# Hybrid decoder layer on one core: three more seven-product pairs in the down projection, part of their block sums made earlier and kept in DRAM, and another order at the end

## The chip, the cores and the metric

One core of one Trainium2 chip. The metric is the device time of one launch in microseconds (us), the median of 3 runs. Engines are called PE (matrix multiply; PEld is its weight load), DVE (vector), ACT (scalar), POOL and SP (the engine whose queue issues nearly all transfers).

## The reference

One decoder layer on x of 256 x 2048 float32, with 16 heads of 128 columns in two groups:

```python
h    = rmsnorm(x, pre_mix_gain)
proj = h @ w_in                                  # 2048 x 6144: q, k, v of 16 heads
o    = concat(stick_breaking(8 heads), dilated(8 heads))   # each head rms-normed
x    = x + rmsnorm(o @ w_out, post_mix_gain)
h    = rmsnorm(x, pre_ffn_gain)
u    = h @ w_up                                  # 2048 x 11008
u    = sum(up[:, j:j + S] * conv_w[j] for j in range(3)) + conv_b     # causal, depthwise
gate, val = split(u)
x    = x + rmsnorm((gelu(gate) * val) @ w_down, post_ffn_gain)        # w_down: 5504 x 2048
```

All is float32, so each matrix is split into a high part (a rounded copy) and a low part (what the rounding left), and a product is three matmuls: high by high, low by high, high by low.

## The kernel before, in words

The weights come as a list of chunks of two tiles of 128x1024 (512 KB each), through five `raw` buffers that SP fills in the list's order. `high` (L88) makes the high part of a tile on ACT, `low` (L93) the low part on DVE by subtracting; there are four buffers for each of the two parts. The chunks are worked in stages: for each of four head groups four value chunks and eight query/key chunks (with the attention of the heads between them), then the output projection, a transition (residual, norm, transposes), 86 chunks of up (43 blocks of 128 columns, gate and value, with convolution and GeLU in `convolved`, L448), and down.

Down (`class Down`, L483) contracts over 43 blocks of 128 rows of w_down, once for each half `cp` of the 2048 output columns. A single block with its 1024 columns is one tile and four products (`ONE`): 12 matmuls of 128x512. Two neighbouring blocks can be a **pair**: a 2x2 block product in the manner of Strassen and Winograd, with seven products for eight (`PAIR`): 21 matmuls for 24. For that it needs sums of y's blocks (made in `convolved` during up) and of the weight's blocks. Of the weight's four 128x512 blocks, tile `ra` holds b12 and b21, tile `rb` the other two, side by side. The sums are T13 = b12 + rb (128x1024, L542) and T24 (two sums of 128x512, L543 and L544, from T13, rb and b21). A pair is then four *units*, each to be split by ACT and DVE and multiplied by PE: T13, T24 and Rb (128x1024, two products each) and Ra (128x512, one product).

`_down_plan` (L40) sets the order. With `NPAIR = 10` there are 10 pairs and 23 singles: in the first half 2 singles, then the pairs with 17 singles spread behind them, then 4 singles; in the second half no single ahead, 19 spread, and the last 4 (`HELD`) are prepared and multiplied at the very end, bank by bank. `run` (L585) prepares (`prepare`, L529: load, sums, high, low) three units ahead of the one that it multiplies. `combine` and `close` add up the seven PSUM banks into `fg`.

The end of `run` takes the last four singles bank by bank. A finished bank is added to `fg` on DVE (`close`, L581), its squares are summed on ACT (`squares`, L397), and it is multiplied by the gain ("take", L583, on POOL or DVE). When the row mean is there (`mean`, L407 to L410; `newton`, L416 and L418), `put` (L616) scales, adds the residual x1b and stores a piece of the output. Rows 0 to 127 are ready first (`put(0, ...)`), rows 128 to 255 (`put(1, ...)`) last.

Each engine executes its own list of instructions in order; a scheduler sets that order from the program and its buffers, except where `pin` keeps the program's order. In the transition `update` (L707) adds the residual in pieces of 128x512, and PE transposes them (L715).

The functions that the change touches:

## Time and profile before

| | |
|---|---|
| runs | 1132.15, 1132.9, 1133.07 us: median 1132.9 |
| the profiled execution | 1131.0 us, of it 1129.2 us from the first to the last instruction |
| busy | PE 1111.9, DVE 856.5, ACT 645.6, POOL 6.3 us |
| clock that PE was granted | 0.996 of full speed over the span |
| transfers | 216.86 MB, 192 GB/s over the span |

The span is from the first to the last instruction of the profiled execution; its own time lies 1.8 us above that, and it was 1.9 us below the median of the runs. Engines run side by side, so busy times don't add up; what an engine's idle time costs depends on whether PE waits for it. The stages stand in the span so: head groups and output projection to about 400 us, the transition to about 410, up to about 893, down from 893 on, and from 1118.7 the end without PE.

### The profile page before, as it was taken

The page shows a single profiled execution, that of the slowest core. Times are in us where ns is not written, and L with a number is a line of the kernel's source. Part 1 is how long each engine was busy: PE and PEld are TensorE (multiplying, and loading weights), DVE is VectorE, ACT ScalarE, POOL GpSimd, SP SyncE. Part 2 cuts the span into 40 slices and gives each one's busy share as a digit, 9 for nine tenths or more (in the row PEclk, how much of TensorE's full clock was granted, in tenths as well). Part 3 has the DMA queues.
Part 4 walks back from the last instruction along what each step waited for, and adds up shares of the span by engine and source line. Part 5 has one row for each costly group of instructions (what it writes and reads, how often), then busy time and mean ns, then how long its engine had stood idle before and what let it go on. Part 6 is the DMA issues. An engine that isn't in the chain of part 4 may idle for free.

```text
span 1129.2 us, 16027 instructions
## 1 busy us (share of the span) xinstructions
PE 1111.9 (98%) x5873; PEld 946.5 (84%) x5873; DVE 856.5 (76%) x1336; ACT 645.6 (57%) x1037; POOL 6.3 (1%) x12
## 2 busy tenths in 40 slices
PE   8999999999999999999999999999999999999996
PEld 6888888888888888888888888888888878887885
DVE  6665565765755488788888887888888898898986
ACT  7555564655654386555555555555555555564563
POOL 0000000000000000000000000000000000000001
PEclk9999999999999999999999999999999999999999
DMA  9764545555555556555555555555555455566555
GB/s 362 250 211 160 186 150 167 169 161 179 165 168 188 185 190 206 187 190 187 188 185 192 184 193 186 189 183 189 186 188 187 153 208 202 204 204 219 208 189 186
DMA packets 59551, 216.86 MB, mean 192 GB/s; under 512 B 6737, under 2 KB 7121, under 8 KB 58705
## 3 DMA queue, kind: packets, MB, share of 16 engines
q1 hardware_dynamic: 59184, 215.77, 57.4%
q8 instruction: 46, 0.75, 0.3%
q14 instruction: 33, 0.26, 0.1%
q10 hardware_dynamic: 288, 0.07, 0.0%
HBM read 211.63 MB, written 4.19 MB: 191 GB/s over the span
## 4 chain that ended last, share of the span: by engine, by line
PE 94%; DVE 3%; ACT 1%; DMA 1%; issue 1%; DVEq 0%; ACTq 0%
PE mmu L101 28%; PE mmu L104 14%; PE mmqk L101 10%; PE p L563 6%; PE p L561 5%; PE p L562 5%; PE mmqk L104 5%; PE mmo L138 3%; PE mmo L134 3%; PE mmo L135 3%; PE mmv L134 3%; PE mmv L135 2%; PE mmv L138 2%; DMA raw<-in_w_v 1%; DVE wl L93 1%
## 5 line engine op out<-in xcount | busy, mean ns | idle before, releaser
L93 DVE TENSOR_TENSOR wl<-raw,wh 128x1024 fp32r<-128x1024 f32 (+1 forms) x387 | 457.8, 1192 | 203.0 <-ACT wh L88 199.8
L88 ACT CAST wh<-raw 128x1024 fp32r<-128x1024 f32 (+1 forms) x387 | 394.2, 1026 | 343.4 <-PE mmu L101 194.5
L101 PE MATMUL mmu<-hT,wh 128*128 128x512 f32 x1344 | 340.5, 395 | 0.2 <-ACT wh L88 0.2
L101 PEld LDWEIGHTS mmu<-hT,wh 128*128 128x128 f32 x1344 | 240.8, 188 | 45.0 <-ACT wh L88 0.4
L104 PEld LDWEIGHTS mmu<-hT,wl 128*128 128x128 f32 x1344 | 184.1, 188 | 15.3
L104 PE MATMUL mmu<-hT,wl 128*128 128x256 f32 x1344 | 187.4, 281 | 0.0
L101 PE MATMUL mmqk<-hT,wh 128*128 128x512 f32 x512 | 132.9, 400 | 0.0
L101 PEld LDWEIGHTS mmqk<-hT,wh 128*128 128x128 f32 x512 | 92.0, 188 | 17.1
L88 ACT CAST wh<-room 128x1024 fp32r<-128x1024 f32 x40 | 42.0, 1050 | 70.3 <-DVE room L542 41.0
L104 PEld LDWEIGHTS mmqk<-hT,wl 128*128 128x128 f32 x512 | 70.0, 188 | 5.8
L563 PE MATMUL p<-wl,yt 128*128 128x512 f32 (+1 forms) x188 | 72.8, 388 | 0.0
L562 PE MATMUL p<-wh,yt 128*128 128x512 f32 (+1 forms) x188 | 72.6, 386 | 0.0
L561 PE MATMUL p<-wh,yt 128*128 128x512 f32 (+1 forms) x188 | 72.6, 386 | 0.0
L104 PE MATMUL mmqk<-hT,wl 128*128 128x256 f32 x512 | 71.2, 281 | 0.0
L563 PE MATMUL p<-wl,yp 128*128 128x512 f32 x140 | 54.8, 395 | 1.0 <-DVE wl L93 1.0
L561 PE MATMUL p<-wh,yp 128*128 128x512 f32 x140 | 55.0, 393 | 0.4 <-ACT wh L88 0.3
L562 PE MATMUL p<-wh,yp 128*128 128x512 f32 x140 | 54.8, 391 | 0.0
L134 PE MATMUL mmv<-wh,hT 128*128 128x512 f32 x128 | 51.7, 406 | 1.5 <-ACT hT L215 1.0
L455 ACT ACTIVATE cv<-u,par 128x256 f32<-128x256 f32 x86 | 51.4, 599 | 2.1 <-DVE u L453 2.1
L93 DVE TENSOR_TENSOR wl<-room,wh 128x1024 fp32r<-128x1024 f32 x40 | 48.8, 1221 | 4.4 <-ACT wh L88 3.6
L135 PE MATMUL mmv<-wh,hT 128*128 128x512 f32 x128 | 50.7, 396 | 0.3 <-DVE hT L236 0.3
L134 PE MATMUL mmo<-wh,mix 128*128 128x512 f32 x128 | 50.6, 396 | 0.0
(173 smaller groups left out, 1223.1 us busy)
## 6 DMA issues: line engine op xcount, KB each, us to landing
raw<-in_w_up SPq DMA_DIRECT2D x172, 512.0 KB, 4.4
raw<-in_w_dn SPq DMA_DIRECT2D x86, 512.0 KB, 4.3
raw<-in_w_qk SPq DMA_DIRECT2D x64, 512.0 KB, 4.1
raw<-in_w_o SPq DMA_DIRECT2D x32, 512.0 KB, 3.6
raw<-in_w_v SPq DMA_DIRECT2D x31, 512.0 KB, 3.7
x<-in_x SPq DMA_DIRECT2D x2, 1024.0 KB, 9.4
x_kept<-x SPq DMA_DIRECT2D x2, 1024.0 KB, 4.4
x1b<-x_kept SPq DMA_DIRECT2D x4, 512.0 KB, 5.3
```

The costliest lines, as they stand in the source:

```text
L88: pin(A.copy(wh, raw))
L93: pin(V.tensor_tensor(wl, raw, wh.bitcast(F32), op=ALU.subtract))
L101: T.matmul(ps, wh[:, j * P:(j + 1) * P], h[:, k, :, :], start=(k == 0), stop=False, skip_group_check=True)
L104: T.matmul(ps[:, 0, :], wl[:, j * P:(j + 1) * P], h[:, k, 0, :], start=False, stop=(k == KT - 1), skip_group_check=True)
L134: T.matmul(ps[t], hi[:, k, tc_], ws, start=(first and i == 0 and j == 0), stop=False)
L135: T.matmul(ps[t], lo[:, k, tc_], ws, start=False, stop=False)
L138: T.matmul(ps[t], hi[:, k, tc_], wl[:, j * 512:(j + 1) * 512], start=False, stop=(last and i == len(parts) - 1 and j == n - 1))
L455: A.activation(cv, u, AF.Identity, scale=cw(2), bias=par[:, P_CB + f:P_CB + f + 1])
L561: T.matmul(ps, yh, wh[:, cs], start=key not in self.begun, stop=False)
L562: T.matmul(ps, yl, wh[:, cs], start=False, stop=False)
L563: T.matmul(ps, yh, wl[:, cs], start=False, stop=self.left[key] == 0)
```

## The change

It has five parts.

1. `NPAIR` is 13, with 17 singles. In the first half 11 singles are spread over 13 pairs (none behind the first and the seventh), in the second half 13 over 13.
2. `presum` is called in each query/key chunk, 26 times. It loads b12 (256 KB) and the pair's other two blocks (512 KB) of w_down, adds them on DVE (128x1024, L535), and stores the result, T13, in DRAM (512 KB, `t13_kept`), one chunk after the sum. Down then loads three tiles for each pair, T13, rb and b21, where it loaded two, and makes only T24's sums (L563, L564), after T13's split.
3. In `convolved` the sums of y's blocks lie in seven rows in another order, so that one cast and one subtraction of 128x896 take the place of two each.
4. `u` and `cv` have single buffers in up, and small tiles move between pools.
5. The end: the takes of the first two banks are made on DVE, those of the last but one and of half of the last on POOL; the residual of rows 0 to 127, columns 1024 to 2047, is copied to PSUM by ACT (`x1p`) and read there; the pieces of `put` for row block 0 are 1024, 256, 256, 512; the order is pinned. In the transition the first update of the second row block is made in two pieces of 256.

```diff
-NPAIR = 10
+NPAIR = 13
...
-        u = pool.tile([P, S], F32, tag=name, name=name)
+        u = pool.tile([P, S], F32, tag=name, name=name, bufs=1)
...
-        cv = phB.tile([P, S], F32, tag=f"cv{s}", name="cv")
+        cv = phB.tile([P, S], F32, tag=f"cv{s}", name="cv", bufs=1)
...
-                a11, a21, a12, a22, s1, s2, s3, s4 = (y[:, j, :] for j in range(8))
+                a11, a21, a12, a22, s1, s2, s4 = (y[:, j, :] for j in range(7))
                 V.tensor_tensor(s1, a22, a21, op=ALU.subtract)
-                V.tensor_tensor(s3, a11, a21, op=ALU.subtract)
+                V.tensor_tensor(a21, a11, a21, op=ALU.subtract)
...
-                for dst, src in ((slice(0, 1), slice(0, 1)), (slice(1, 7), slice(2, 8))):
-                    A.copy(yp[0][:, m, dst, :], y[:, src, :])
-                    V.tensor_tensor(yp[1][:, m, dst, :], y[:, src, :], yp[0][:, m, dst, :].bitcast(F32), op=ALU.subtract)
+                A.copy(yp[0][:, m, :, :], y)
+                V.tensor_tensor(yp[1][:, m, :, :], y, yp[0][:, m, :, :].bitcast(F32), op=ALU.subtract)
...
+                    if kind == "pair":
+                        self.tiles += [kept[cp, j], a["w_dn"][cp, :, at + 1024:at + 2048], a["w_dn"][cp, :, at + 512:at + 1024]]
+                        self.presums.append((a["w_dn"][cp, :, at:at + 512], self.tiles[-2], kept[cp, j]))
...
+        def presum(self):
+            if self.summed and self.summed[0][1]:
+                t13, _, kept = self.summed.pop(0)
+                nc.sync.dma_start(kept, t13)
+            for i, (t13, done, kept) in enumerate(self.summed):
+                if not done:
+                    b12 = self.b12.rearrange("p (o c) -> p o c", o=1).broadcast_to([P, 2, 512])
+                    two = t13.rearrange("p (o c) -> p o c", o=2)
+                    V.tensor_tensor(two, b12, two, op=ALU.add)
+                    self.summed[i] = (t13, True, kept)
+            if self.presums:
+                one, two, kept = self.presums.pop(0)
+                self.b12 = apool.tile([P, 512], F32, tag="b12", name="b12")
+                nc.sync.dma_start(self.b12, one)
+                t13 = apool.tile([P, HALF], F32, tag="t13", name="t13")
+                nc.sync.dma_start(t13, two)
+                self.summed.append((t13, False, kept))
...
-                    rb = self.raws[first + 1]
-                    if what == "T13":
-                        t13, t24 = room[:, 3, 0:HALF], room[:, 3, HALF:]
...
-                        V.tensor_tensor(two(t13), b12, two(rb), op=ALU.add)
+                    rb, b21 = self.raws[first + 1], self.raws[first + 2]
+                    if what == "T24":
+                        t24 = room[:, 3, j % 2 * HALF:(j % 2 + 1) * HALF]
                         V.tensor_tensor(t24[:, 0:512], t13[:, 0:512], rb[:, 512:], op=ALU.add)
-                        V.tensor_tensor(t24[:, 512:], t24[:, 0:512], ra[:, 512:], op=ALU.add)
-                    src = self.sums[what]
+                        V.tensor_tensor(t24[:, 512:], t24[:, 0:512], b21, op=ALU.add)
+                        self.t24 = t24
+                    src = {"T13": t13, "T24": self.t24, "Rb": rb, "Ra": b21}[what]
                 self.parts.append(low(src, high(src)))
...
-            for b in (2, 3):
-                products(b)
-                self.close(1, b)(G)
-            r = rows.newton(*rows.mean(0))
+            products(2)
+            take2 = self.close(1, 2)
+            take2(V)
+            products(3)
+            take3 = self.close(1, 3)
+            for i in range(2):
+                A.copy(x1p[i], x1s[1][:, i * 512:(i + 1) * 512])
+            pinned[0] = True
+            mean = rows.mean(0)
+            pin(take3(V))
+            r = rows.newton(*mean)
             products(4)
+            take4 = self.close(1, 4)
             put(0, 0, 1024, r)
-            take = self.close(1, 4)
-            put(0, 1024, 1536, r)
-            take(G)
             products(8, 0, 256)
-            self.close(1, 8, 0, 256)(G)
+            take8 = self.close(1, 8, 0, 256)
+            pin(take4(G))
+            put(0, 1024, 1280, r)
             products(8, 256, 512)
-            take = self.close(1, 8, 256, 512)
+            take9 = self.close(1, 8, 256, 512)
+            pin(take8(G))
+            put(0, 1280, 1536, r)
             put(0, 1536, 2048, r)
             mean = rows.mean(1, 5)
-            take(V)
+            pin(take9(V))
             r = rows.newton(*mean)
...
+            down.presum()
...
-                update(1, 0)
+                update(1, 0, 0, 256)
+                update(1, 0, 256, 512)
```

What this does to the engines' lists, at three places. First DVE in the second half of down, around the splits of one pair (`raw` and `room` are the source of a split, `wl` its low part). Before (the first row is two singles, the fifth T13 and T24):

```order
L93 TENSOR_TENSOR wl<-raw,wh 128x1024 x2
L542 TENSOR_TENSOR room<-raw 128x1024
L543 TENSOR_TENSOR room<-room,raw 128x512
L544 TENSOR_TENSOR room<-room,raw 128x512
L93 TENSOR_TENSOR wl<-room,wh 128x1024 x2
L93 TENSOR_TENSOR wl<-raw,wh 128x1024
L93 TENSOR_TENSOR wl<-raw,wh 128x512
```

and now (the first row is one single and T13):

```order
L93 TENSOR_TENSOR wl<-raw,wh 128x1024 x2
L563 TENSOR_TENSOR room<-raw 128x512
L564 TENSOR_TENSOR room<-room,raw 128x512
L93 TENSOR_TENSOR wl<-room,wh 128x1024
L93 TENSOR_TENSOR wl<-raw,wh 128x1024
L93 TENSOR_TENSOR wl<-raw,wh 128x512
```

The sum L542 is gone, T13's low has moved ahead of T24's sums, and between T24's sums and T24's low stands no other instruction.

Second the SP queue in the query/key chunks of the second head group. Before, it held the weights alone:

```order
L78 DMA raw<-in_w_qk 128x1024 x10
L78 DMA raw<-in_w_v 128x1024
L679 DMA gbc<-in_gpost 128x2048
L78 DMA raw<-in_w_v 128x1024 x7
L78 DMA raw<-in_w_qk 128x1024 x16
```

and now, two chunks of it (`t_kept<-t_...` is the store of a T13, `b_...` the load of b12):

```order
L530 DMA t_kept<-t_1188 128x1024
L540 DMA b_1296<-in_w_dn 128x512
L78 DMA raw<-in_w_qk 128x1024
L542 DMA t_1298<-in_w_dn 128x1024
L78 DMA raw<-in_w_qk 128x1024
L530 DMA t_kept<-t_1242 128x1024
L540 DMA b_1365<-in_w_dn 128x512
L78 DMA raw<-in_w_qk 128x1024
L542 DMA t_1367<-in_w_dn 128x1024
L78 DMA raw<-in_w_qk 128x1024
```

Each chunk has a store and two loads more, and the load of the other two blocks goes into the buffer from which that chunk's store is read (two `t13` buffers).

Third DVE at the end, from the last bank but two to the last mean. Before:

```order
L581 TENSOR_TENSOR room<-p_9746,room 128x512
L407 TENSOR_SCALAR rj,rv<-ssd 128x4
L416 SCALAR_TENSOR_TENSOR rq<-rr,rv 128x1
L418 SCALAR_TENSOR_TENSOR rs<-rq,rr 128x1
L616 SCALAR_TENSOR_TENSOR room<-room,rs,x1b 128x1024
L581 TENSOR_TENSOR room<-p_9745,room 128x512
L616 SCALAR_TENSOR_TENSOR room<-room,rs,x1b 128x512
L581 TENSOR_TENSOR room<-p_10540,room 128x256
L616 SCALAR_TENSOR_TENSOR room<-room,rs,x1b 128x512
L581 TENSOR_TENSOR room<-p_10541,room 128x256
L407 TENSOR_SCALAR rj,rv<-ssd 128x5
```

and now (`x1p` is the residual in PSUM):

```order
L604 TENSOR_TENSOR room<-room 128x512
L416 SCALAR_TENSOR_TENSOR rq<-rr,rv 128x1
L418 SCALAR_TENSOR_TENSOR rs<-rq,rr 128x1
L602 TENSOR_TENSOR room<-p_9927,room 128x512
L641 SCALAR_TENSOR_TENSOR room<-room,rs,x1b 128x1024
L602 TENSOR_TENSOR room<-p_10760,room 128x256
L641 SCALAR_TENSOR_TENSOR room<-room,rs,x1p 128x256
L602 TENSOR_TENSOR room<-p_10761,room 128x256
L641 SCALAR_TENSOR_TENSOR room<-room,rs,x1p 128x256
L641 SCALAR_TENSOR_TENSOR room<-room,rs,x1p 128x512
L407 TENSOR_SCALAR rj,rv<-ssd 128x5
```

The last 256 columns are added after one `put` of 1024 and one of 256, where it was after 1024, 512 and 512, and the puts that stand beside POOL's takes read the residual from PSUM.

## Rows read from the trace of the kernel before

**Rows 1.** The profile's page: busy time, share of the span and instructions of each engine; the chain that ended last by engine; two transfer rows (name, count, KB each, median us from issue to landing).

```profile
PE 1111.9 (98%) x5873; PEld 946.5 (84%) x5873; DVE 856.5 (76%) x1336; ACT 645.6 (57%) x1037; POOL 6.3 (1%) x12
...
PE 94%; DVE 3%; ACT 1%; DMA 1%; issue 1%; DVEq 0%; ACTq 0%
...
raw<-in_w_dn SPq DMA_DIRECT2D x86, 512.0 KB, 4.3
...
out<-room SPq DMA_DIRECT2D x1, 512.0 KB, 2.6
```

**Rows 2.** Busy time by stretch: window in us and its length, then PE, PEld, DVE, ACT and POOL busy with instructions, granted clock, DMA share, GB/s. The stretches are the first loads, the query/key chunks of one head group, the transition, most of up, and the two halves of down.

```profile
10.00:35.00 25.00, 24.68 (x112) 19.82 (x111) 16.40 (x23) 17.95 (x25) 0.51 (x1) 1.00 1.01 412
...
108.00:160.00 52.00, 52.00 (x309) 45.86 (x308) 32.22 (x52) 29.36 (x55) 0.00 (x0) 1.00 0.53 170
...
404.00:410.00 6.00, 5.74 (x37) 5.54 (x37) 5.86 (x15) 5.45 (x16) 0.00 (x0) 0.74 0.39 141
432.00:884.00 452.00, 452.00 (x2572) 394.61 (x2571) 369.40 (x605) 261.31 (x405) 0.00 (x0) 1.00 0.58 188
893.00:1006.00 113.00, 112.10 (x487) 90.58 (x486) 102.36 (x109) 63.27 (x69) 0.00 (x0) 1.00 0.57 200
1006.00:1118.00 112.00, 111.48 (x497) 91.18 (x496) 98.72 (x108) 61.78 (x75) 2.59 (x2) 1.00 0.58 197
```

**Rows 3.** Groups of equal instructions in down (893 to 1118.4): line, engine, operation, output from input, shapes, count, busy us, mean ns of one, idle time before them and what ended it.

```profile
L93 DVE TENSOR_TENSOR wl<-raw,wh 128x1024 fp32r<-128x1024 f32 x64 | 77.3, 1219 | 5.1 <-ACT wh L88 4.7
...
L88 ACT CAST wh<-room 128x1024 fp32r<-128x1024 f32 x40 | 42.0, 1050 | 70.3 <-DVE room L542 41.0 <-PE p L563 11.1 <-DVE room L544 10.7
...
L542 DVE TENSOR_TENSOR room<-raw 128x1024 f32<-128x1024 f32 x20 | 24.5, 1223 | 10.6 <-DMA raw<-in_w_dn 9.0 <-PE mmu L104 1.5
L543 DVE TENSOR_TENSOR room<-room,raw 128x512 f32<-128x512 f32 x20 | 13.8, 690 | 0.5
...
L93 DVE TENSOR_TENSOR wl<-raw,wh 128x512 fp32r<-128x512 f32 x20 | 13.7, 683 | 0.0
...
L581 DVE TENSOR_TENSOR room<-p,room 128x512 f32<-128x512 f32 x7 | 4.5, 684 | 2.6 <-PE p L563 2.6
```

**Rows 4.** The timeline around one pair of the first half: start us, us, engine, line, operation, count, and in brackets the idle time before it and what ended it. A row with a count of 3 or 4 is as many instructions back to back.

```profile
932.56 0.68 DVE L543 TENSOR_TENSOR room<-room,raw 128x512 f32<-128x512 f32 x1
933.16 1.22 DVE L93 TENSOR_TENSOR wl<-room,wh 128x1024 fp32r<-128x1024 f32 x1
934.30 0.68 DVE L544 TENSOR_TENSOR room<-room,raw 128x512 f32<-128x512 f32 x1
935.09 1.05 ACT L88 CAST wh<-room 128x1024 fp32r<-128x1024 f32 x1 [2.42 <-DVE room L544]
936.17 1.23 DVE L93 TENSOR_TENSOR wl<-room,wh 128x1024 fp32r<-128x1024 f32 x1 [1.19 <-ACT wh L88]
937.32 4.09 DVE L93 TENSOR_TENSOR wl<-raw,wh 128x1024 fp32r<-128x1024 f32 x4
937.46 0.51 PE L563 MATMUL p<-wl,yp 128*128 128x512 f32 x1 [0.23 <-DVE wl L93]
...
938.96 0.39 PE L563 MATMUL p<-wl,yp 128*128 128x512 f32 x1
...
941.71 0.39 PE L563 MATMUL p<-wl,yt 128*128 128x512 f32 x1
```

**Rows 5.** The same view: places in down at which PE waited, and DVE's wait behind one of them.

```profile
907.84 0.51 PE L561 MATMUL p<-wh,yp 128*128 128x512 f32 x1 [0.27 <-ACT wh L88]
...
964.88 1.22 DVE L93 TENSOR_TENSOR wl<-room,wh 128x1024 fp32r<-128x1024 f32 x1 [1.19 <-ACT wh L88]
...
966.16 0.50 PE L563 MATMUL p<-wl,yp 128*128 128x512 f32 x1 [0.26 <-DVE wl L93]
...
1026.88 0.51 PE L563 MATMUL p<-wl,yp 128*128 128x512 f32 x1 [0.52 <-DVE wl L93]
```

**Rows 6.** The same view at the end: PE's last matmul, DVE and POOL.

```profile
1115.48 0.68 DVE L416 SCALAR_TENSOR_TENSOR rq<-rr,rv 128x1 f32<-128x1 f32 x1 [0.51 <-ACT rr L410]
...
1116.39 1.29 DVE L616 SCALAR_TENSOR_TENSOR room<-room,rs,x1b 128x1024 f32<-128x1024 f32 x1
1117.60 0.68 DVE L581 TENSOR_TENSOR room<-p,room 128x512 f32<-128x512 f32 x1
1118.20 0.74 DVE L616 SCALAR_TENSOR_TENSOR room<-room,rs,x1b 128x512 f32<-128x512 f32 x1
...
1118.42 0.28 PE L563 MATMUL p<-wl,yt 128*128 128x256 f32 x1
...
1119.11 2.40 POOL L583 TENSOR_TENSOR room<-room 128x512 f32<-128x512 f32 x2 [2.96 <-ACT jks L397]
...
1119.19 1.74 DVE L616 SCALAR_TENSOR_TENSOR room<-room,rs,x1b 128x512 f32<-128x512 f32 x1
1120.85 0.41 DVE L581 TENSOR_TENSOR room<-p,room 128x256 f32<-128x256 f32 x1
1121.89 0.16 DVE L407 TENSOR_SCALAR_CACHE_REDUCE rj<-ssd 128x5 f32<-128x5 f32 x1 [0.64 <-ACT jks L397]
```

**Rows 7.** The same view in the transition: the updates, and PE's first transpose of the second row block.

```profile
401.51 1.41 DVE L707 SCALAR_TENSOR_TENSOR x<-mg,rs,x 128x512 f32<-128x512 f32 x2
...
402.31 0.99 PE L715 MATMUL pth<-ident,x 128*128 128x128 f32 x5 [1.81 <-DVE x L707]
```

More of the change, by code (lines that the diff above doesn't have):

```diff
@@ L190, in layer_kernel @@
     A.preload_act_table_set("natural_log_exp_and_others")
-    gpre = cpool.tile([P, KT], F32, name="gpre")
     par = cpool.tile([P, P_END], F32, name="par")
@@ L199, in layer_kernel @@
     cst = apool.tile([P, C_END - P], F32, name="cst", bufs=1)
+    gpre = apool.tile([P, KT], F32, name="gpre", bufs=1)
     x1 = apool.tile([P, 2, D], F32, name="x1", bufs=1)
@@ L220, in layer_kernel @@
     nc.scalar.dma_start(gpre, a["par"][:, P_PRE:P_PRE + KT])
-    warm = cpool.tile([P, 512], BF16, name="warm")
+    warm = apool.tile([P, 512], BF16, name="warm", bufs=1)
     V.memset(warm, 0.0)
@@ L394, in squares @@
         def squares(self, ps, t, c):
-            jk = wpool.tile([P, 512], BF16, tag="jks", name="jks", bufs=1)
+            jk = (phB or apool).tile([P, 512], BF16, tag="pair" if phB else "jks", name="jks", bufs=1, padded_shape=[P, 7 * P * 2] if phB else None)
             jk = jk[:, 0:ps.shape[-1]]
@@ L469, in convolved @@
             if odd == 0:
-                pair[0] = phB.tile([P, 8, P], F32, tag="pair", name="pair", bufs=1)
+                pair[0] = phB.tile([P, 7, P], F32, tag="pair", name="pair", bufs=1)
             y = pair[0]
@@ L490, in layer_kernel @@
         PAIR = (
-            ("T13", ((5, 3, 0), (7, 5, 512))),
-            ("T24", ((6, 4, 0), (4, 2, 512))),
+            ("T13", ((5, 4, 0), (7, 1, 512))),
+            ("T24", ((6, 5, 0), (4, 3, 512))),
             ("Rb", ((1, 0, 0), (3, 6, 512))),
-            ("Ra", ((2, 1, 0),)),
+            ("Ra", ((2, 2, 0),)),
         )
@@ L498, in __init__ @@
         def __init__(self):
-            self.units, self.tiles = [], []
+            self.units, self.tiles, self.presums, self.summed = [], [], [], []
+            kept = nc.dram_tensor("t13_kept", (2, NPAIR, P, HALF), F32, kind="Internal").ap()
             for cp in range(2):
@@ L504, in __init__ @@
                     n = 2 if kind == "pair" else 1
-                    for _ in range(n):
+                    if kind == "pair":
+                        self.tiles += [kept[cp, j], a["w_dn"][cp, :, at + 1024:at + 2048], a["w_dn"][cp, :, at + 512:at + 1024]]
+                        self.presums.append((a["w_dn"][cp, :, at:at + 512], self.tiles[-2], kept[cp, j]))
+                    else:
                         self.tiles.append(a["w_dn"][cp, :, at:at + 1024])
-                        at += 1024
+                    at += 1024 * n
                     if kind == "pair":
@@ L512, in __init__ @@
                         self.units.append((cp, "one", j, first, self.ONE))
-            self.raws, self.parts, self.sums = [], [], {}
+            self.raws, self.parts, self.t24 = [], [], None
             self.left = {}
@@ L531, in prepare @@
                 self.load(first + 5)
[L532 removed]
+                t13 = self.raws[first]
                 if what == "one":
[L534 removed]
+                    src = t13
                 else:
[L536 to L542 removed]
+                    rb, b21 = self.raws[first + 1], self.raws[first + 2]
+                    if what == "T24":
+                        t24 = room[:, 3, j % 2 * HALF:(j % 2 + 1) * HALF]
                         V.tensor_tensor(t24[:, 0:512], t13[:, 0:512], rb[:, 512:], op=ALU.add)
[L544 to L545 removed]
+                        V.tensor_tensor(t24[:, 512:], t24[:, 0:512], b21, op=ALU.add)
+                        self.t24 = t24
+                    src = {"T13": t13, "T24": self.t24, "Rb": rb, "Ra": b21}[what]
                 self.parts.append(low(src, high(src)))
@@ L612, in run @@
                 nc.sync.dma_start(x1s[h], x1_kept[h // 2 * P:(h // 2 + 1) * P, h % 2 * HALF:(h % 2 + 1) * HALF])
+            x1p = [ps_at.tile([P, 512], F32, tag="at", name="x1p") for _ in range(2)]
             def put(t, lo, hi, r):
                 x = x1s[2 * t + lo // HALF][:, lo % HALF:(hi - 1) % HALF + 1]
-                V.scalar_tensor_tensor(fg[:, t, lo:hi], fg[:, t, lo:hi], r, x, op0=ALU.mult, op1=ALU.add)
+                if t == 0 and lo >= HALF:
+                    x = x1p[lo // 512 - 2][:, lo % 512:(hi - 1) % 512 + 1]
+                pin(V.scalar_tensor_tensor(fg[:, t, lo:hi], fg[:, t, lo:hi], r, x, op0=ALU.mult, op1=ALU.add))
                 nc.sync.dma_start(out[t * P:(t + 1) * P, lo:hi], fg[:, t, lo:hi])
@@ L641, in run @@
                 put(1, lo, hi, r)
+            pinned[0] = False
     down = Down()
@@ L704, in layer_kernel, with update @@
                 col = lambda c: slice(c * 512, (c + 1) * 512)
-                def update(t, c):
-                    pin(V.scalar_tensor_tensor(x1[:, t, col(c)], mg[:, t, col(c)], r[t], x1[:, t, col(c)],
-                                               op0=ALU.mult, op1=ALU.add))
+                def update(t, c, lo=0, hi=512):
+                    cs = slice(c * 512 + lo, c * 512 + hi)
+                    pin(V.scalar_tensor_tensor(x1[:, t, cs], mg[:, t, cs], r[t], x1[:, t, cs], op0=ALU.mult, op1=ALU.add))
                 def turn(t, b):
```

12 lines of the change are left out of this document (4 added, 8 removed).

## The prediction

> **What bounds the kernel now.** I read the page first: PE is busy in 98% of the span and makes up 94% of the chain that ended last, DVE 76% [rows 1]. So a change pays by taking matmuls from PE, provided that the other engines still keep it fed, or by shortening the stretch at the end in which PE is done. Then the table by stretch [rows 2], because the 76% of DVE is a mean: in the query/key chunks it is busy 32.22 of 52 us (62%), in up 369.40 of 452 (82%), in the two halves of down 102.36 of 113 and 98.72 of 112 (91% and 88%). PE is full in the first two; in down it lacks 0.9 and 0.5 us by its busy time. Then the groups of down for the price of one instruction [rows 3], the timeline around a pair for the order in which they wait for each other [rows 4, 5], and the timeline at the end and in the transition [rows 6, 7]. The sum below is made against the profiled execution, 1131.0 us (span 1129.2 and 1.8 around it); the median of the runs, 1132.9, lies 1.9 above it, so I add 1.9 at the end. About 0.2% (2.27 us) is what a measurement of this kernel can tell from no change.
>
> **Matmuls.** Twelve matmuls of 128x512 start between 938.96 and 941.71 [rows 4]: 0.229 us each, although a row shows 0.39 (they overlap). A pair of blocks costs PE 21 x 0.229 = 4.81 us, a single 12 x 0.229 = 2.75. Three pairs more save 3 x 3 matmuls in each half of the columns: 18 x 0.229 = **-4.1 us**, if PE is fed. For what there is now, 10 pairs and 23 singles twice make 222.7 us; the stage takes 893.0 to 1118.7, 225.7, so it already loses about 3.
>
> **DVE in down.** This is where I expect most of those 4.1 to be lost. Back to back, a 128x1024 low or sum costs 1.14 (933.16 to 934.30), a 128x512 one 0.60 (four lows of 1024, 512, 1024, 1024 take 4.09, which is 3 x 1.16 and 0.60) [rows 4]. The two sums of T24 depend on each other and take 1.41 together (0.72 and 0.69, the busy 0.69 of one with what lies between).
> Before, a pair costs DVE L542 1.14, two sums 1.38, lows of T13, T24, Rb and Ra 1.14 x 3 + 0.60, together 6.5; with gaps of the dependent sums I take 6.76. T13's cast on ACT (1.05) lies beside the T24 sums, so DVE rarely waits for it.
> After, L542 is gone, but T13's low comes first, and then T24's two sums directly ahead of T24's low. That low needs ACT's cast of the finished sum, and DVE has nothing to do in between. The trace of before shows this very order three times: L544 at 934.30, the cast at 935.09 for 1.05, the low at 936.17 after 1.19 us of idle [rows 4], again at 964.88 [rows 5]. So a pair costs 1.14 + 1.41 + 1.19 + 1.14 + 1.14 + 0.60 = 6.62: the 1.14 of L542 comes back as a wait.
> First half: 13 x 6.62 + 11 x 1.14 = 98.6 us on DVE against 13 x 4.81 + 11 x 2.75 = 92.8 on PE, a lack of 5.8. Second half: 13 x 6.62 + 13 x 1.14 = 100.9, and four closes and four takes at about 0.6 (the 0.68 of L581 [rows 3], back to back) = 4.8, so 105.7 against 13 x 7.56 = 98.3, a lack of 7.4. Four part buffers, one being multiplied and one being written, let PE run on for about two finished units, 2 x 1.4 = 2.8 us per half. That leaves (5.8 - 2.8) + (7.4 - 2.8) = 7.6 us of waiting. By the same count before, the first half has 10 x 6.76 + 17 x 1.14 = 87.0 against 94.9, no lack, and it still lost about 3 at single places: 0.27 at 907.84, 0.26 at 966.16, 0.52 at 1026.88 [rows 5], the last two behind such a cast. I take 7.6 as the whole of the new waits, since the old ones are mostly of the same kind and would be counted twice: **+4.5** against the 3.1 of now. Ends: 0 if the lists interleave better than my mean, and +7.6 if the old waits come on top.
> Two gains I leave out and keep as bounds: DVE waited 9.0 us at L542 for the tile `rb` [rows 3]; and the new third tile, b21, is needed soon after T13's. A tile lands 4.3 us after its issue [rows 1], about a single and a unit of PE's time, and five raw buffers hold the next pair; 0 us here, with up to 0.8 (9.0 over its 11 waits) at a few pairs the other way.
>
> **Presum.** 26 of 32 query/key chunks get 1.31 MB of transfers (0.26 + 0.52 loaded, 0.52 stored) and a sum of 1.22 us [rows 3] each. A chunk takes about 6.75 us, so DVE goes from 62% to some 80%, which is what it bears in up with PE full (82%) [rows 2]. Transfers go from 170 GB/s by 1.31 MB / 6.75 us = 194 to 364, where the first loads show 412 carried [rows 2]. On the SP queue the load of the next blocks waits until the store from that buffer has landed (a 512 KB store takes 2.6 [rows 1]), and the chunk's second weight tile is queued behind it. Five raw buffers are two and a half chunks, 16 us, of lead; I take **+0.3**, between 0 and the price of the second rival on the slow side.
>
> **Up** changes by three more pairs' y sums (some 1.4 us of DVE each) and a merged cast and subtraction; that is 4 us in a stretch of 452 with 82 us of DVE free [rows 2], hidden. If single buffers made DVE wait for ACT there, that slack is what it would eat first. **Transition:** PE waits 1.81 us for the first update, of which one takes 0.7 [rows 7]; with two pieces of 256 the first transposes can start some 0.3 earlier: **-0.2**, between 0 and -1.7, the latter only if it spared the drop of the granted clock that follows (0.74 in 404 to 410, so part of it at half speed).
>
> **The end.** PE's last matmul starts at 1118.42, but its bank is added at 1120.85, behind puts of 1024, 512 and 512, of which the last takes 1.74 where its like takes 0.74, beside POOL's takes (1119.11 to 1121.5) [rows 6]. After: the row's factor is there at about 1116.4 as now (a take of 0.6 more on DVE ahead of it, but L416 took 0.68 beside POOL and ought to take 0.22 as a little one does). Then on DVE: add 0.60, put 1.2, add 0.35, put 0.42, add: the last bank is done near 1119.4, two puts of 0.4 and 0.7 follow, and the mean stands at about 1120.4 for 1121.89 now: **-1.5**. Beside POOL the add at 1120.85, which reads PSUM, took its normal 0.41 [rows 6], and all puts that stand beside POOL now read PSUM; if they stretched like the 1.74 one, 1.0 of it would be lost. Bounds -1.9 and 0.
>
> **Sum:** -4.1 + 4.5 + 0.3 - 0.2 - 1.5 = -1.0. 1131.0 - 1.0 + 1.9 = **1131.9 us**, which is no difference that can be told. This case's own range: 1130.7 to 1135.1.
>
> **The rivals.**
> *DVE keeps up (faster).* The T24 wait is absorbed by the singles between the pairs; only the present 3.1 us of waits stay. Then -4.1 + 0.3 - 0.2 - 1.5 = -5.5: 1127.4. For it: DVE loses its 9.0 us of waits for `rb`, and in the three places where this order stood before PE lost only 0.2 to 0.5 us. Against it: the per-pair sum exceeds PE's time for a pair and a single (7.76 against 7.56) even without a close. Half of it would be 1129.6, still faster.
> *The T24 wait reaches PE at every pair (slower).* The place is L564, ACT's cast, T24's low. If two finished units are not there when DVE stops, PE waits 0.34 on the mean of 0.23, 0.26 and 0.52 [rows 4, 5] at each of 26 pairs, 8.8, on top of the 2.1 of today that lie elsewhere: +7.8 for my +4.5, 1135.2. It decides where lead is below some 2.4 us when T13's low ends; pairs with no single behind them favour it.
> *Transfers in query/key (slower).* The mixed loads and stores are carried slower than the loads of [rows 2]. 364 is 12% below 412; at 15% less than 412 (350 GB/s) 52 us of such chunks (364 x 52 = 18.9 MB) need 18.9 / 350 = 54.1, +2.1 for each of 3.25 groups: +6.8, 1138.7. Against it: no row of before carries stores for that long, but 412 leaves room. The Trainium skill (DMA: Bandwidth & Descriptors, Where 436 GB/s comes from) gives about 358 GB/s as the limit for traffic between HBM and a core; by that rule the chunks would take 52.8 for 52, +2.6 in all, 1134.2. The 412 of this trace stands above it, so it does not bind a lone core's loads; whether it does with stores among them no row here shows.
> *It doesn't do what it says.* The order shows L542 gone and 18 matmuls fewer; what could fail is the end, if ACT's two copies to PSUM delay the squares and with them the factor: 1133.4.
>
> **Chances.** Forecast (about the same) 0.41; DVE keeps up, wholly or half, 0.37; T24's wait at every pair 0.12; transfers 0.07; the end without gain 0.03 (also the same in size, within 0.2%). Of the forecast's own range a little lies beyond 1135.17, and little below 1130.6: faster 0.38, same 0.42, slower 0.20. The range that should hold 8 in 10 runs from the first rival with a little more of its waits gone, 1126.8, to the second with a margin for query/key, 1136.4; the transfers' full price lies outside.
>
> **What would show it.** Right: down (from its first matmul to its last) within 1 us of its 225.7 now, PE waiting there 6 to 9 us, mostly for lows (L93) and casts; an idle of about 1.2 ahead of the T24 lows in most pairs; query/key stages as long as now with 340 to 370 GB/s; the last mean some 2.0 us behind the start of the last matmul, 3.5 now. Wrong: down shorter by 3 us or more, or a DVE group without that idle; PE idle in query/key; a drop of the granted clock in down, as the transition has one after PE's wait.

## The result, and the profile after

The change is slower: 1136.96 us median of 6 runs (1135.06 to 1139.5) against 1132.57 of 6 of the kernel before in the same comparison; the ratio is 1.0044 (95% interval 1.0034 to 1.0055), so 3.9 to 6.2 us. The profiled executions are 1137.09 and 1131.0 us, their spans 1134.8 and 1129.2. I split the spans by the starts of PE's own matmuls:

| stretch | before | after | difference | predicted |
|---|---|---|---|---|
| start to the first matmul of the output projection (head groups) | 308.65 | 316.97 | +8.3 | +0.3 |
| from there to the first matmul of down (output, transition, up) | 584.34 | 583.99 | -0.35 | -0.2 |
| first to last matmul of down | 225.43 | 224.59 | -0.8 | +0.4 (-4.1 + 4.5) |
| last matmul to the end | 10.79 | 9.29 | -1.5 | -1.5 |
| span | 1129.2 | 1134.8 | +5.6 | -1.0 |

One row is wrong, by 8.0 us; down gives 1.2 of it back, and the other two agree within 0.2. Of the 8.3, 0.5 stood already after the first loads, before presum's first transfer (28.1 us). The page after (columns as in [rows 1]):

```profile
PE 1111.2 (98%) x5855; PEld 938.0 (83%) x5855; DVE 880.2 (78%) x1369; ACT 651.7 (57%) x1038; POOL 3.4 (0%) x10
...
PE 83%; DMA 7%; DVE 5%; ACT 3%; issue 2%; SPq 1%; DVEq 0%; ACTq 0%
...
raw<-in_w_qk SPq DMA_DIRECT2D x64, 512.0 KB, 6.3
...
t_kept<-t SPq DMA_DIRECT2D x26, 512.0 KB, 6.6
```

PE's share is the same 98%, since the rows round; but the chain now holds 7% of transfers and 1% of the SP queue, where it had 1% and none [rows 1]. Busy time by stretch after (columns as in [rows 2]):

```profile
108.00:160.00 52.00, 50.47 (x299) 44.16 (x297) 35.97 (x55) 27.34 (x52) 0.00 (x0) 1.00 0.91 307
213.00:265.00 52.00, 50.06 (x268) 42.31 (x267) 37.98 (x78) 29.57 (x68) 0.00 (x0) 1.00 0.94 318
901.00:1013.00 112.00, 110.52 (x476) 86.71 (x475) 95.39 (x108) 64.97 (x75) 0.00 (x0) 1.00 0.71 237
1013.00:1126.00 113.00, 112.73 (x494) 88.50 (x492) 98.84 (x117) 65.44 (x86) 0.83 (x1) 1.00 0.67 224
```

In 108 to 160 PE was full before [rows 2]; now it lacks 1.5 us, while transfers went from 170 to 307 GB/s, not to the 364 that I had asked of them. The SP queue shows why. Its timeline over two query/key chunks, and two later rows (start, us, line, transfer):

```profile
126.46 0.33 SPq L542 DMA_DIRECT2D t<-in_w_dn  x1
126.88 0.38 SPq L78 DMA_DIRECT2D raw<-in_w_qk  x1
127.37 0.37 SPq L530 DMA_DIRECT2D t_kept<-t  x1
127.79 0.42 SPq L540 DMA_DIRECT2D b<-in_w_dn  x1
128.31 0.89 SPq L78 DMA_DIRECT2D raw<-in_w_qk  x1
134.50 0.33 SPq L542 DMA_DIRECT2D t<-in_w_dn  x1
...
141.72 0.33 SPq L542 DMA_DIRECT2D t<-in_w_dn  x1
...
149.68 0.33 SPq L542 DMA_DIRECT2D t<-in_w_dn  x1
150.10 0.38 SPq L78 DMA_DIRECT2D raw<-in_w_v  x1
```

SP issues five transfers in 2.7 us and then stands until 134.50, because the next one (L542) goes into the buffer whose store (127.37) has not landed. Such rounds take 7.6 us on the mean here (from 118.98 over 126.46 and 134.50 to 141.72); a chunk of matmuls took 6.4 before (eight from 107.31 to 158.25). So the weight tiles fall behind: the one issued at 100.2 us before is issued at 105.1 now, the one of 142.8 at 157.8. SP's waits from 60 to 309 us (who waited for what: us in all, times, longest), after, and then the longest before:

```profile
SPq L542 <- DMA t_kept<-t: 93.8, 20, 5.9
SPq L78 <- DVE wl L93: 45.0, 21, 5.0
```

```profile
SPq L78 <- DVE wl L93: 139.7, 45, 4.2
```

Before, SP waited there for DVE alone, to free a buffer, that is, it was early. Now it waits 4.7 us in 20 chunks for its own store. The tiles' lead shows the same: before, a tile lay in its buffer 7.5 to 11.8 us between its landing and ACT's cast (casts from 108 to 160); after, from 118 to 173, 0.8 us at most. How PE comes to pay, at the end of the second head group:

```profile
156.03 1.05 ACT L88 CAST wh<-raw 128x1024 fp32r<-128x1024 f32 x1 [1.02 <-DMA raw<-in_w_v]
157.12 1.23 DVE L93 TENSOR_TENSOR wl<-raw,wh 128x1024 fp32r<-128x1024 f32 x1 [1.15 <-ACT wh L88]
159.34 1.05 ACT L88 CAST wh<-raw 128x1024 fp32r<-128x1024 f32 x1 [1.64 <-DMA raw<-in_w_v]
159.39 0.61 DVE L319 TENSOR_SCALAR on<-po,rr 128x128 f32<-128x128 f32 x2
159.88 0.50 PE L323 MATMUL pt<-ident,on 128*128 128x128 f32 x2 [1.53 <-DVE on L319]
```

The weight tile issued at 150.10 is late, ACT's cast at 156.03 waits for it, DVE's low for the cast, and an attention instruction (L319) stands behind that low in DVE's queue (five small ones between them, back to back); PE waits for it. The trace names DVE as the releaser; the cause is four steps back.

Down went as worked out. Its groups, and one pair (columns as in [rows 3] and [rows 4]):

```profile
L93 DVE TENSOR_TENSOR wl<-room,wh 128x1024 fp32r<-128x1024 f32 x26 | 31.9, 1226 | 28.8 <-ACT wh L88 27.6 <-PE p L583 1.2
```

```profile
949.28 0.69 DVE L564 TENSOR_TENSOR room<-room,raw 128x512 f32<-128x512 f32 x1
950.08 1.05 ACT L88 CAST wh<-room 128x1024 fp32r<-128x1024 f32 x1 [3.33 <-DVE room L564]
951.16 1.23 DVE L93 TENSOR_TENSOR wl<-room,wh 128x1024 fp32r<-128x1024 f32 x1 [1.19 <-ACT wh L88]
```

The 1.19 us of idle ahead of T24's low, three times before [rows 4, 5], is now there at nearly every pair: 27.6 us. And the end (columns as in [rows 6]):

```profile
1125.55 0.28 PE L584 MATMUL p<-wl,yt 128*128 128x256 f32 x1
1126.16 0.42 DVE L602 TENSOR_TENSOR room<-p,room 128x256 f32<-128x256 f32 x1
1126.50 1.13 DVE L641 SCALAR_TENSOR_TENSOR room<-room,rs,x1p 128x256 f32<-128x256 f32 x2
1127.55 0.15 DVE L407 TENSOR_SCALAR_CACHE_REDUCE rj<-ssd 128x5 f32<-128x5 f32 x1
```

The last mean stands 2.0 us behind the start of the last matmul, where it was 3.5 [rows 6], and the puts beside POOL took their normal time.

### The profile page after: what moved, and what is told of

It is laid out like the page before. It is cut to its first block, busy times and chain, and to the rows that moved or that the text cites. A ratio compares the mean times of both kernels' runs of the same rounds, so it can differ in the third digit from the quotient of the medians.

```text
span 1134.8 us, 16276 instructions
## 1 busy us (share of the span) xinstructions
PE 1111.2 (98%) x5855; PEld 938.0 (83%) x5855; DVE 880.2 (78%) x1369; ACT 651.7 (57%) x1038; POOL 3.4 (0%) x10
## 4 chain that ended last, share of the span: by engine, by line
PE 83%; DMA 7%; DVE 5%; ACT 3%; issue 2%; SPq 1%; DVEq 0%; ACTq 0%
PE mmu L101 28%; PE mmu L104 14%; PE mmqk L101 7%; PE p L582 5%; PE p L583 5%; PE p L584 5%; PE mmqk L104 4%; PE mmo L134 3%; PE mmo L135 3%; PE mmo L138 3%; DVE wl L93 2%; DMA t_kept<-t 2%; PE mmv L134 2%; PE mmv L135 2%; PE mmv L138 2%
## 5 line engine op out<-in xcount | busy, mean ns | idle before, releaser
L93 DVE TENSOR_TENSOR wl<-raw,wh 128x1024 fp32r<-128x1024 f32 (+1 forms) x413 | 482.4, 1186 | 159.3 <-ACT wh L88 157.2
L88 ACT CAST wh<-raw 128x1024 fp32r<-128x1024 f32 (+1 forms) x413 | 414.1, 1021 | 309.5 <-PE mmu L101 189.7
L582 PE MATMUL p<-wh,yp 128*128 128x512 f32 x182 | 74.0, 406 | 1.6 <-ACT wh L88 1.5
L88 ACT CAST wh<-room 128x1024 fp32r<-128x1024 f32 x26 | 27.2, 1048 | 81.5 <-DVE room L564 74.8
L583 PE MATMUL p<-wh,yp 128*128 128x512 f32 x182 | 71.5, 393 | 0.0
L584 PE MATMUL p<-wl,yp 128*128 128x512 f32 x182 | 63.9, 393 | 0.0
L93 DVE TENSOR_TENSOR wl<-room,wh 128x1024 fp32r<-128x1024 f32 x26 | 31.9, 1226 | 28.8 <-ACT wh L88 27.6
L582 PE MATMUL p<-wh,yt 128*128 128x512 f32 (+1 forms) x140 | 53.9, 385 | 0.0
L583 PE MATMUL p<-wh,yt 128*128 128x512 f32 (+1 forms) x140 | 53.9, 386 | 0.0
L584 PE MATMUL p<-wl,yt 128*128 128x512 f32 (+1 forms) x140 | 53.8, 386 | 0.0
```

Of the source, the lines that this page charges most:

```text
L88: pin(A.copy(wh, raw))
L93: pin(V.tensor_tensor(wl, raw, wh.bitcast(F32), op=ALU.subtract))
L582: T.matmul(ps, yh, wh[:, cs], start=key not in self.begun, stop=False)
L583: T.matmul(ps, yl, wh[:, cs], start=False, stop=False)
L584: T.matmul(ps, yh, wl[:, cs], start=False, stop=self.left[key] == 0)
```

## The experiments

All medians are beside the kernel before on the same chip (1131.9 to 1132.3 us there); stretches are those of the profiled executions. "Query/key" is the time to the first matmul of the output projection, 308.65 before and 316.97 in the change; it varies by up to 2 us with the first loads.

**e1, the change without presum.**

```diff
-            down.presum()
...
+                        V.tensor_tensor(two(t13), b12, two(rb), op=ALU.add)
```

> The change without presum: 13 pairs, the end, the transition and up as in the change, but T13 is summed in down as before and two tiles are loaded for each pair. In the change's profile the query/key chunks are 8.0 us longer than before, down 0.8 shorter, the end 1.5 shorter, the transition 0.3 shorter. If the 8.0 come from presum (queue or transfers), they are gone here: query/key as long as before within 0.5 us. In down DVE then has 13 x 6.76 + 11 x 1.14 = 100.4 us for PE's 92.8 in the first half and 107.5 for 98.3 in the second, so I expect down 2 to 8 us longer than before, and 1133 to 1139 in all. Rival: the pairs' sums hide as well as in the change; then down is about 1 shorter than before and the time near 1130.

1138.61 us (ratio 1.0053, 1.0038 to 1.0068). Query/key 310.17: the loss is presum's. Down 232.59, 8.0 longer than in the change: 13 pairs need presum, and it is worth 8 us there.

**e2, the end and the small parts alone.**

```diff
-NPAIR = 13
+NPAIR = 10
...
-            down.presum()
```

> Ten pairs as before and no presum: of the change only the end, the transition, the order of y's sums and the single buffers in up are left. In the change's profile the end is 1.5 us shorter and the stretch from the last product of the output projection to down about the same. So 1130.3 to 1131.0, 1.2 to 1.9 below before, with the end (from PE's last matmul) 9.2 to 9.6 for 10.8 and down as long as before (225.4). Rival: the end's gain depends on down having ended late for DVE; then the end is 10.3 or more and the time that of before.

1130.53 (0.9986, 0.9977 to 0.9995). The end is 8.93 us, 1.9 shorter, query/key 308.53. Down is 226.79, 1.4 longer than before (1.2 of it where its second half begins, 1008 to 1012 us), which I had not expected and whose cause stays open; the total came out as expected.

**e3, presum's transfers issued by POOL.**

```diff
-                nc.sync.dma_start(kept, t13)
+                nc.gpsimd.dma_start(kept, t13)
```

(and so for both loads.)

> The change with presum's loads and stores issued by POOL instead of SP; same bytes, same buffers, same sums. Theory A: the loss in query/key is the order on the SP queue (the load of the next blocks waits for a store that takes 6.6 us to land, and a weight tile is queued behind it). Then query/key loses 2 us or less instead of 8, and the time is about 1130 to 1132. Theory B: it is the rate (the engines of the transfers are 91% busy at 307 GB/s there); then the weight tiles land as late as in the change, 6 us or more, and the time stays at 1135 to 1138.

1197.73 (1.0581), query/key 380.75. Both theories missed. Up to 381 us POOL waited 82.0 us for the stores, and DVE, whose sums the order still put early, 66.1 us for the loads, up to 7.4 at a time, with lows and attention behind them; the granted clock was 0.86 and 0.89 in 60 to 108 and 108 to 160. The edit brought waits of its own on POOL and DVE, so it settles neither theory.

**e4, no stores.**

```diff
-                t13, _, kept = self.summed.pop(0)
-                nc.sync.dma_start(kept, t13)
+                self.summed.pop(0)
```

> The change without the stores of T13: its blocks are loaded and summed in query/key as in the change, and down loads the unsummed blocks in T13's place (so the sum is left out of the result). Per chunk 0.79 MB for 1.31 and no wait for a store. Theories A and B both expect query/key back to within 1 us of before, 1129 to 1130 in all. Theory C, that DVE's extra sum of 1.2 us in each chunk pushes the attention's instructions behind it, expects 5 us or more of the 8 to stay: 1134 or more.

1130.7 (0.9986, 0.9977 to 0.9995); query/key 310.75. The 26 sums on DVE, with presum's loads, cost 2 us at most; the other 6 come with the stores (their bytes or the waits for them, this run doesn't part the two).

**e5, presum spread over more chunks.**

```diff
+        if i >= 8 and kind in ("v", "qk", "out"):
+            down.presum()
```

(with the sum in every second call, and store and next loads in the others.)

> The change with presum spread over the value, query/key and output chunks from the ninth chunk on: one pair per two chunks, and the load of the next blocks goes into the buffer whose store was issued two chunks earlier. Half the bytes per chunk, and no load right behind its own store. Theories A and B expect most of the 8 us back, 1129.5 to 1131.5; if DVE's sums are what costs, they cost as much here: 1135 or more.

1133.03 (1.0011, 1.0001 to 1.0020). The scheduler moved the loads forward again: 306 to 319 GB/s as in the change. SP no longer waited for a store, but 44.2 us for the loads and sums ahead of its stores, and DVE stood 20.9 us at its sums, while no tile of the second group came late (4.5 us or more from landing to cast). Query/key 315.31 in the profiled execution (1135.45 us).

**e6, spread and held in program order.**

```diff
-                    V.tensor_tensor(two, b12, two, op=ALU.add)
+                    tc.keep_in_program_order(V.tensor_tensor(two, b12, two, op=ALU.add))
```

(and so for presum's store and loads.)

> As the run that spread presum, whose lists turned out not to be spread (the loads had moved forward, 306 to 319 GB/s as in the change, and DVE waited 20.9 us for them); here each load, store and sum is held behind what the program has before it on its engine, so that every four weight tiles on SP are followed by one store and one pair of loads, into output chunks too. Theory A (SP waits for a store, weight tiles late) and theory D (DVE waits at its sum for a load, and the attention's instructions behind it come late) both expect query/key within 1.5 us of before at 230 to 270 GB/s, and 1129.5 to 1131.5 in all. If DVE's 26 sums cost by themselves, query/key stays 4 us or more longer and the time is 1133 or more.

**1129.52** (0.9980, 0.9971 to 0.9990), query/key 308.52. The same sums and bytes at half the rate cost PE nothing:

```profile
108.00:160.00 52.00, 52.00 (x308) 45.91 (x307) 36.29 (x56) 29.28 (x55) 0.00 (x0) 1.00 0.82 284
```

**e7, the sum on POOL.**

```diff
-                    V.tensor_tensor(two, b12, two, op=ALU.add)
+                    G.tensor_tensor(two, b12, two, op=ALU.add)
```

> The change with presum's sum on POOL instead of DVE; transfers, queue and buffers as in the change. Theory D (DVE waits at the sum for its load with the attention's instructions behind it) expects half or more of the 7 us of query/key back: 1130 to 1134. Theory A (weight tiles late, since SP waits for the store) expects the loss to stay, 1136 or more; a POOL sum of 2.6 us or so also makes the store later, and stretches DVE's instructions that read two operands from SBUF (one of 512 took 1.74 us beside POOL for 0.74), so it may well be more, 1140.

1149.59 (1.0157). Inconclusive: POOL's sum takes 2.54 us, and some of DVE's instructions stretch beside it (the 128x512 product L329 takes 1.31 us on the mean and 2.92 at most for 0.69 before, the lows 1.34 and 3.41 for 1.22), so the edit brought a cost of its own.

**e9, e6 with one T13 buffer.** SP waits for the store again, at half the rate.

```diff
-                t13 = apool.tile([P, HALF], F32, tag="t13", name="t13")
+                t13 = apool.tile([P, HALF], F32, tag="t13", name="t13", bufs=1)
```

> The kernel with presum spread and held in order (half the bytes per chunk, query/key as long as before), but with one buffer for T13 instead of two: every load of the next blocks goes into the buffer that was just stored, so SP waits for each store again, at the lower rate, with weight tiles queued behind. If that wait by itself is what costs in the change (theory A), half or more of the 7 us come back: query/key 3 to 7 us longer than before, 1133 to 1137. If it takes the higher rate too (the raw buffers' lead covers a wait of 4.4 us once in two chunks), query/key stays within 1 us of before and the time at 1129 to 1130.5.

1129.7 (0.9977, 0.9967 to 0.9988), query/key 309.33. Its waits:

```profile
SPq L538 <- DMA t_kept<-t: 34.3, 19, 3.8
```

1.8 us once in two chunks is paid from the lead. So a wait behind a store is no loss in itself.

**e13, the change's rate and buffers, held in program order.** As e6's edit, on the change.

> The change with presum's loads, stores and sums held behind what the program has before them, one pair in each query/key chunk as in the change: the full rate and the wait for the store stay, but DVE's sums stand behind the chunk's own sum and no longer ahead of it. If what costs is DVE waiting at its sum ahead of the attention's instructions, query/key loses 2 us or less and the time is 1129 to 1131.5. If it is the rate or the queue, 5 us or more of the 7 stay: 1134 to 1138.

1138.53 (1.0051, 1.0035 to 1.0068), query/key 318.60; SP waits 101.7 us for stores. DVE waited 3.8 us for the sums' loads, where it was 12.5 in the change, and nothing came back: the place of the sums was not the cause.

**e14, e6 with one store more in 40 chunks.**

```diff
+            if self.call <= 40:
+                tc.keep_in_program_order(nc.sync.dma_start(self.extra[self.call], x1[:, self.call % 2, 0:HALF]))
```

> The kernel with presum spread and held in order, and one store of 512 KB more in each of 40 value and query/key chunks, from the residual x, on which nothing waits (their target is not read): about 1.18 MB of presum and extra transfers per chunk where the change has 1.31 and the spread kernel 0.65. If the rate by itself costs (306 to 319 GB/s was all that the transfers reached there), weight tiles land late and 4 to 8 us come back: 1133.5 to 1138. If the rate costs only together with a queue that stands behind a store, query/key stays within 1.5 us of the spread kernel and the time at 1129.5 to 1131.

1136.38 (1.0042, 1.0027 to 1.0057). The total says rate, the trace says otherwise:

```profile
60.00:108.00 48.00, 48.00 (x264) 41.16 (x263) 32.68 (x61) 28.81 (x62) 0.00 (x0) 1.00 0.98 347
108.00:160.00 52.00, 52.00 (x308) 45.88 (x307) 35.96 (x56) 29.24 (x56) 0.00 (x0) 1.00 0.96 343
160.00:213.00 53.00, 53.00 (x282) 45.09 (x281) 33.23 (x54) 26.84 (x50) 0.00 (x0) 1.00 0.93 325
...
60.00:80.00 20.00, 20.00 (x125) 17.81 (x124) 14.98 (x30) 13.29 (x31) 0.00 (x0) 1.00 1.00 374
...
248.00:268.00 20.00, 18.59 (x93) 15.31 (x92) 11.10 (x18) 9.59 (x18) 0.00 (x0) 1.00 1.02 401
```

More than the change's 302 to 307 was carried with PE full; the matmul that before starts at 232.5 starts at the same time, 7.7 later in the change. The weight tiles took even longer to land than in the change, and yet ACT hardly waited for them. The landing in 108 to 160 and ACT's waits for tiles from 60 to 309, first in the change, then in e14:

```profile
raw<-in_w_qk SPq DMA_DIRECT2D x9, 512.0 KB, 6.3
...
ACT wh L88 <- DMA raw<-in_w_v: 12.5, 9, 3.3
ACT wh L88 <- DMA raw<-in_w_qk: 9.4, 6, 2.2
```

```profile
raw<-in_w_qk SPq DMA_DIRECT2D x8, 512.0 KB, 8.9
...
ACT wh L88 <- DMA raw<-in_w_v: 0.6, 1, 0.6
```

Before had no such wait. So what the change pays for is a tile that is issued late, not one that lands slowly. e14's loss comes later, 4 us by the output projection and 4 more in it. By 309 SP had stood 75.0 us in 15 waits for sums ahead of their stores (up to 6.8 each), 43.7 of it from 108 to 213, where PE lost nothing: there SP issued sixteen tiles in 52.4 us (106.2 to 158.6), which in the change took 59.3 (106.5 to 165.7), and ACT cast the same sixteen in 53.2 before. The first 4 us of e14's loss are hardly late tiles: PE waited 3.0 us for casts, and ahead of the longest of these waits (1.41 us, at 266.23) the tile had landed 4.9 us before, while its cast stood in ACT's list behind a copy (L708) that waited 4.7 us for PE. In output ACT waited 5.3 us for tiles; whether that is the queue or the rate, the run doesn't tell.

**e15, e13 with the waiting load issued by POOL.**

```diff
-                tc.keep_in_program_order(nc.sync.dma_start(t13, two))
+                nc.gpsimd.dma_start(t13, two)
```

> The run with presum held in program order at the full rate (1138.5), with one edit: the load of the pair's other two blocks, the one that waits for the store, is issued by POOL; the store, b12 and the weight tiles stay on SP. Theory A (the queue): SP no longer stands behind the store, the weight tiles are issued as their buffers come free, and query/key loses 3 us or less instead of 8 to 9: 1130.5 to 1133.5. Theory B (the amount of traffic): 6 us or more stay, 1136 or more. What could spoil it: store, load and sum of one buffer then follow each other in 6.6 + 4.5 + 1.2 us or more, with 13.5 us for two chunks, and DVE would wait at the sums.

1145.64 (1.0116, 1.0098 to 1.0134), query/key 325.95. SP no longer stands at the load, but the spoiler named in the expectation came true: SP waits for the load and the sum ahead of its next store, and DVE at its sum:

```profile
DVE t L535 <- DMA t<-in_w_dn: 21.2, 11, 4.3
```

The second group's tiles are no longer late (5.6 us or more from landing to cast), and the loss is larger: with two buffers at one pair per chunk, load, sum and store follow each other with no slack, and whichever engine stands in that loop delays what is queued behind it.

**e8, T24's sums written ahead of T13's split** (on the change), and **e10, the same on e6 with T13's low held behind both sums**, and **e11, e10 with 10 pairs**.

```diff
-                    if what == "T24":
+                    if what == "T13":
```

```diff
-                self.parts.append(low(src, high(src)))
+                wh = high(src)
+                pinned[0] = what == "T13"
+                self.parts.append(low(src, wh))
+                pinned[0] = False
```

> The change with T24's two sums ahead of T13's split, as before, so that ACT's cast of T24 runs beside DVE's low of T13. In the change DVE idles 27.6 us in 26 waits for that cast, and down takes 224.6 us where 218.6 would be full. If that idle is what keeps PE waiting, it goes, and down takes 220 to 222.5: 1133 to 1135 in all. Rival: the sums now need the third tile earlier and T13's low comes later by 1.4 us, so PE waits for T13 instead; then down stays within 1 us of 224.6 and the time at 1137.

> Presum spread and held in order, and T24's sums ahead of T13's split with T13's low held behind both sums, so that DVE has 1.14 us to do while ACT casts T24. DVE's time for a pair falls from 6.62 to about 5.4, and PE's 4.81 and 2.75 become the bound: down 219.5 to 221.5 for 225.0, 1124.5 to 1127 in all. Rival: PE then waits for T13, whose low comes 1.4 us later; down 223 or more, 1128 or more.

> The same with 10 pairs. If PE bounds down in both, 18 matmuls more cost their 4.1 us: down 223 to 225, 3.5 to 4.5 above the run with 13 pairs. If DVE still bounds down with 13, this one is as fast or within 1.5 us of it.

e8: 1134.95 (1.0022, 1.0007 to 1.0037), down 221.91, 2.7 shorter than in the change, query/key 319.48: DVE makes T13's low between the two sums, though the idle of 1.2 stays. e10: 1138.22 (1.0056), down 231.17, the rival and worse: the idle is gone, and DVE stands at the sums for tiles instead (e10's waits in down):

```profile
DVE room L560 <- DMA raw<-in_w_dn: 19.9, 16, 1.8
...
DVE room L561 <- DMA raw<-in_w_dn: 7.5, 10, 1.4
```

e11: 1139.94 (1.0063), 1.7 above e10, which is less than the runs of either scatter (3.6 and 4.5), down 232.86 with 41.7 us of DVE's waits for tiles at L560: in this order tiles bound it, not PE, and three pairs show no clear gain.

**e12, e6 with e8's edit.**

> Presum spread and held in order (1129.5), and T24's sums written ahead of T13's split but not held, as in the run that shortened down by 2.7 us. If the two add up: query/key as before, down about 222, the end 9.5: 1126 to 1127.5. If the tiles land too late for the earlier sums, as in the run with the held order (down 231), down is 225 or more and the time 1129.5 or more.

**1126.73 us** (0.9952, 0.9937 to 0.9967), the best of all: query/key 309.02, down 221.14, the end 9.41. Its down has the tile waits of e10 no more:

```profile
DVE wl L93 <- ACT wh L88: 25.6, 23, 1.2
...
DVE room L560 <- DMA raw<-in_w_dn: 1.6, 2, 1.3
```

## Why the prediction was wrong

- **The step that failed is "Presum".** It put +0.3 where the profile has +8.3. It saw the right instruction ("the load of the next blocks waits until the store from that buffer has landed ..., and the chunk's second weight tile is queued behind it"), and mis-sized it twice. It took a store's landing from the end of the kernel, 2.6 us [rows 1], where SP has nothing else; among five transfers issued in 2.7 us it took 6.6. And it set the raw buffers' lead of 16 us against one wait, though the wait comes in each chunk: a round of 7.6 us against 6.4 (it had 6.75 for a chunk) uses up a us or more of lead per chunk (the tiles' issue fell 10 us further behind in seven chunks, from 4.9 at 105.1 to 15.0 at 157.8), so the loss shows first at the end of the second group (158 us) and then in the third.
- **The rival "transfers in query/key"** named the place and the sign and had 0.07, but rate as its mechanism. e14 carried 343 to 347 GB/s in two stretches without loss, e9 shows that the wait alone is free at half the rate, e6 that the sums and bytes at half the rate are free. The price that this rival took, 350 GB/s at most, did not bind either: e14 moved 374 from 60 to 80 us, with PE full, and 401 from 248 to 268. The Trainium skill (DMA: Bandwidth & Descriptors, Where 436 GB/s comes from) gives about 358 GB/s as the limit for traffic between HBM and a core; e14's 374 and 401 stand above it, with stores among the loads, which the prediction had left open. Shown is that the loss needs presum's stores (e4), goes with half the rate (e6), and is not the rate or the landing of the tiles (e14, up to 213 us, where the change had lost 4.5 after its first loads): it takes a queue that issues its tiles more slowly than they are used, here by a wait for its own store in every chunk. e13 agrees: there ACT waited 36.8 us for tiles. e5 and e15 lose by another way, DVE standing at its sums; ACT waited for tiles not at all in e5 and 4.7 us in e15. A third buffer there, the direct test, was not tried.
- **DVE in down** was right in mechanism, and nearly in size: 3.3 us of new waits for my 4.5 (-0.8 for +0.4), with the 1.19 of idle at nearly every pair, and 7.75 us from one T24 low to the next with a single between them, for the 7.76 worked out. By the price of a matmul PE loses 224.6 - 218.6 = 6.0 us there, the low end of the 6 to 9 named as the sign; its weight loads waited for casts (11.5 us in 40 waits at L582) and hardly for lows (0.9 in 3). e8 and e12 confirm that DVE's loop takes the gain: with 0.13 us less of it per pair (6.49 for 6.62 between the T24 lows of two pairs with no single between them; 26 pairs), down is 2.7 to 3.9 shorter. The rival that DVE keeps up was wrong by the same row, and the 7.8 us of the rival that has PE wait at every pair did not come.
- **Leaving out tile waits** was right for the change (3.8 us on ACT, none on DVE), but only in its order: in e10 they are 27.4 us on DVE.
- **Matmuls and the end** came as worked out: 18 matmuls fewer, and -1.5. e2 has the end without pairs and presum: 8.93, and 1.4 us below before in all.
- **Up and the transition** are right in the sum, -0.35 for -0.2, but partly by luck. The first matmul of up stands 3.82 us behind the last of the output projection, 4.16 before, which is the 0.3 foreseen. The drop of the granted clock was spared as well (1.00 in 411 to 417, where 404 to 410 before had 0.74), for which the bound was -1.7, but it brought nothing: PE waited 1.6 us for ACT's `hT` instead, 0.3 before, and up took 0.7 longer. The output projection took 0.7 less, which no term had; why stays open.

## What to carry to other kernels

Price a transfer's wait by how often it comes per round, not against the lead: a queue whose round (issues, plus the wait for its own store) is longer than the consumer's round loses the difference each time, and the lead only delays it. Take a landing time from a row with as many transfers issued around it as the change will have, and ask of work moved into a "free" stage what stands in order behind its waits. If a stage has slack in bytes, spread the work and hold it in program order: not held, the same spread loads were moved together again (e5).

## What was not expected of the hardware

- A 512 KB store landed 2.6 us after its issue at the kernel's end, 4.4 at 267 to 284 GB/s (e6), and 6.6 at 302 to 318 among bunched issues; weight tiles went with it from 3.8 to 6.0 (query/key) and from 3.7 to 7.1 (value). The rate alone does not set it: in e14, at 321 to 349 GB/s, T13's stores, which SP issued after it had stood, landed in 3.8, and the extra stores, issued among the tiles, in 7.6 to 9.1.
- Loads and stores together reached 347 GB/s over 48 us with PE full, and 401 over 20 us (e14).
- A sum of 128x1024 on POOL took 2.54 us against 1.22 on DVE, and beside it DVE's products and lows took either their usual time or up to 2.92 us for 0.69 and 3.41 for 1.22 (e7).
